# Residual scale and shift deferred through DRAM, and operand sums on VectorE alone

## The chip, the cores and the metric

The kernel runs on one core of one Trainium2 chip. The metric is device time of one execution in microseconds (us); below, the median of three runs. TensorE (PE) multiplies, VectorE (DVE), ScalarE (ACT) and GpSimd (POOL) do elementwise work, SyncE (SP) issues the DMAs.

## The reference, cut to what matters

Two blocks run one after the other over 1024 tokens of width 1024. The change touches the middle of the first (its feed-forward part) and the feed-forward part of the second.

```python
y = hybrid_mixer(h, ...)                      # ends in  o @ w_o
x = layer_norm(ALPHA * x + (1.0 + gt_a) * y, ln1_g, ln1_b)
h = x * (1.0 + sc_f) + sh_f
u = causal_dwconv(h @ w_up, conv_w) + conv_b  # w_up: 1024 x 5632
gate, val = jnp.split(u, 2, axis=-1)
y = (jax.nn.silu(gate) * val) @ w_down
x = layer_norm(ALPHA * x + (1.0 + gt_f) * y, ln2_g, ln2_b)
...
hid = jnp.square(jax.nn.relu(rmsnorm(h, norm_mlp_g) @ w_mlp_in))   # second block
h = h + hid @ w_mlp_out
```

The layer norm's result serves twice: with gain and shift folded into `sc_f` and `sh_f` it is the operand `h` of `w_up`, and scaled by ALPHA it is the residual of the last line of the block.

## The kernel before, in words

All matmuls are fp32, each done as three: an operand is split into a rounded part (hi, a cast) and a remainder (lo, a subtraction), and `mm3` multiplies lo by hi, hi by lo and hi by hi. `split` casts on ScalarE (L430) or VectorE (L432) and subtracts on VectorE (L433) unless told otherwise. Tokens come in two halves of 512; an operand of a half is `op[hf]`, a pair (`oph`, `opl`) of eight slabs of 128x512.

The order of the work comes from generators ("streams") that yield estimated times; `Order` interleaves them, and the tile framework turns what they emit into one in-order queue per engine. Pages of 128x1024 come from an arena; a stream waits with `need` until enough are free.

`out_proj` multiplies by `w_o` and adds the gated result to the residual (`add_gated`: VectorE multiplies, L1716; the add L1717 is GpSimd's for three column blocks of four). After each half it spawns `norm1`: statistics, the normalised row (ScalarE, L642), transposes on TensorE (L419), scale and shift into a buffer (ScalarE, L675) and the split into the operand, all in `to_op`, which has two buffers of half a page and gives the remainder of even slabs to GpSimd. Then `norm1` scales the four rows by `ln1_g` (VectorE, L1761), shifts them by `ln1_b` (GpSimd, L1762), both times ALPHA (L1738), and stores them to `res_d` (L1775). `fix` reads them back in the down stage, hundreds of us later.

`ffn` multiplies by `w_up`. `g_two` does the first two pairs of column blocks in the plain way: products of the first half (op0), then those of the second (op1), with the conv taps L574 on VectorE. The other blocks follow in `st_up` in the manner of Strassen: per two pairs 14 steps of 12 matmuls ("a round"), seven products p = 1, 2, 5, 6, 7, 3, 4, each of two pairs. Products 5, 6, 7 and 4 use sums of the quarters of h, which `x_ops` makes: `ts[0]` (p = 5, step 4), `ts[1]` (p = 6), and two more, called t3 and t4 here (p = 7 and 4), which replace the spare weight ring and a part of op1. Each step's weight is split just ahead, four steps in hand (L433, `wl`). When p = 3 and p = 4 are added up (L1959, L1961), the conv taps of the pair (ScalarE L2088, VectorE L2090 and L2062) and the recombination L1998 to L2001 follow on VectorE, and SyncE stores the result (L2003, L2004). `mlp` of the second block makes its sums with `x_ops` as well.

`x_ops` before: per group of slabs GpSimd takes the hi parts (L1793, L1798, L1802), VectorE the lo parts (L1794, L1795, L1799, L1803) and the remainders.

Of the kernel before, what the change touches and what calls it, by code (L numbers as in the profile page):

```python
# [10 lines left out]
F32 = mybir.dt.float32  # L11
# [3 lines left out]
OP = mybir.AluOpType  # L15
# [4 lines left out]
P = 128  # L20
T = 1024
D = 1024
# [288 lines left out]
class Kern:  # L311
# [348 lines left out]
    def to_op(self, srcs, op, sc, bi=None, kts=range(KT)):  # L660
# [4 lines left out]
        for i, k in enumerate(kts):  # L665
# [3 lines left out]
            if bi is None:  # L669
                nc.scalar.activation(h[:, k, :n], ps[:, :n], AF.Copy, scale=sc(k))  # L670
                nc.vector.scalar_tensor_tensor(l[:, k, :n], ps[:, :n], sc(k), h[:, k, :n].bitcast(F32), op0=OP.mult,
                                               op1=OP.subtract)
            else:
                f = self.opf[i % len(self.opf)]
                nc.scalar.activation(f[:, :n], ps[:, :n], AF.Identity, scale=sc(k), bias=bi(k))  # L675
                self.split(f[:, :n], h[:, k, :n], l[:, k, :n], hi_eng=nc.vector, lo_eng=nc.vector if i % 2 else nc.gpsimd)
            self.psg(ps)
# [1033 lines left out]
    def add_gated(self, hf, c):  # L1711
        def f(t0, ps):
            V, G = self.nc.vector, self.nc.gpsimd
            y = self.yt[:, 4 * hf + t0:4 * hf + t0 + 2, c * 256:(c + 1) * 256]
            t = p3(self.gy[c % 2].ap, 256)[:, t0:t0 + 2]
            V.tensor_tensor(t, ps, self.gt[:, None, c * 256:(c + 1) * 256].to_broadcast([P, 2, 256]), OP.mult)  # L1716
            (V if c == 3 else G).tensor_tensor(y, t, y, OP.add)  # L1717
        return f

    def out_proj(self):  # L1720
# [7 lines left out]
        for hf in range(2):  # L1728
# [4 lines left out]
            if hf == 0:  # L1733
                yield self.need(2)
                self.l1 = A.full(self.ypages), A.full(self.ypages)
                for r, n in zip(self.l1, ("ln1_g", "ln1_b")):
                    self.row_of(r.ap, I[n][0])
                    G.tensor_scalar(r.ap, r.ap, ALPHA, None, op0=OP.mult)  # L1738
                hs = self.const.tile([P, 8], F32, name="h2s")
# [9 lines left out]
    def norm1(self, hf):  # L1749
# [3 lines left out]
        yield from self.ln_rows(rows)  # L1753
        yield self.need(0, 2)
        of = A.half(), A.half()
        self.opf = [h.ap for h in of]
        yield from self.to_op(rows, self.op[hf], lambda k: hs[:, k:k + 1], lambda k: hb[:, k:k + 1])
        self.o.set(self.h2[hf])
        A.give(*of)
# [5 lines left out]
        if hf:  # L1765
            A.give(*self.l1)

# [9 lines left out]

    def x_ops(self, ready, free, evs):


        V, G, A = self.nc.vector, self.nc.gpsimd, self.A
# [4 lines left out]
        t3, t2 = [], []  # L1786
        for j in range(4):
            h11, l11, h12, l12 = [f(x[:, j]) for x in (h0, l0, h1, l1)]
            h22, l22 = f(h1[:, 4 + j]), f(l1[:, 4 + j])
            yield self.need(0, 2)  # L1790
            ap, bp = A.half(), A.half()
            a, b = ap.ap, bp.ap
# [3 lines left out]
            yield 0.4  # L1796
            self.split(a, self.ts[0][0][:, j], self.ts[0][1][:, j])
            G.tensor_tensor(b, h22, a, sub)  # L1798
            V.tensor_tensor(b, b, l22, add)  # L1799
            yield 0  # L1800
            self.split(b, self.ts[1][0][:, j], self.ts[1][1][:, j])
            G.tensor_tensor(a, b, h11, sub)  # L1802
            V.tensor_tensor(a, a, l11, sub)  # L1803
            t3.append(ap)
            t2.append(bp)
            yield 1.54
        yield free
        h3, l3 = [t.rearrange("p (k n) -> p k n", n=512) for t in self.wring[1 - self.wi % 2]]
        for j in range(4):
            self.split(t3[j].ap, h3[:, j], l3[:, j], lo_eng=G if j % 2 else V)  # L1810
            A.give(t3[j])
            yield 1.67
        self.o.set(evs[0])
        for j in range(4):
            b = t2[j].ap
            G.tensor_tensor(b, f(h0[:, 4 + j]), b, sub)
            V.tensor_tensor(b, b, f(l0[:, 4 + j]), add)
            self.split(b, h1[:, j], l1[:, j])
            A.give(t2[j])
            yield 2  # L1820
        self.o.set(evs[1])
# [228 lines left out]
    def ffn(self, sc):  # L2050
# [70 lines left out]
        yield self.h2[0]  # L2121
        self.o.spawn(self.x_ops(self.h2[1], two, tev))
        parts = []
# [958 lines left out]
    def main(self):  # L3082
        G = self.nc.gpsimd
        with ExitStack() as sc:
            ps = self.inner(sc, "pa", 9)
            self.mx = sc.enter_context(self.pool("mx"))
# [3 lines left out]
            self.hgain = self.const.tile([P, 2], F32, name="hgain")  # L3090
            self.x2_d = self.dram.tile([T, D], F32, name="x2_d")
            self.res_d = self.dram.tile([T, D], F32, name="res_d")
            self.g_d = self.dram.tile([32, P, T], F32, name="g_d")
# [74 lines left out]
```

## Time and profile before

| | us |
|---|---|
| median of three runs | 2745.09 (2742.69 to 2749.76) |
| the profiled execution | 2746.61 |
| its span | 2744.9 |
| PE busy | 2585.3 (94%), 13053 matmuls |
| DVE busy | 1972.6 (72%) |
| ACT busy | 1316.8 (48%) |
| POOL busy | 528.3 (19%) |

The span is what the trace covers; the profiled execution's own time holds 1.7 us around it. The granted TensorE clock was 0.982 of full speed over the span. Shares over the span are means over stages: read a stage from windows of it, and a wait from the engine that ended it.

### The profile page before, as it was taken

How to read it: one execution, taken by the hardware profiler on the slowest of the kernel's cores; microseconds unless marked ns; L12 is line 12 of the kernel's file. 1: busy time of each engine (PE TensorE's matmuls, PEld its weight loads, DVE VectorE, ACT ScalarE, POOL GpSimd, SP SyncE). 2: the span in 40 equal slices, each digit the busy share in tenths (PEclk: the TensorE clock that was granted, in tenths of full speed). 3: DMA queues.
4: the chain of work that ended last, by engine and by line, in shares of the span. 5: the costliest groups of instructions: out<-in, count | busy, mean ns of one | idle time of the engine just before them, and what ended most of it. 6: DMA issues, size and time to landing. Idle time of an engine off the chain costs nothing.

```text
span 2744.9 us, 36015 instructions
## 1 busy us (share of the span) xinstructions
PE 2585.3 (94%) x13053; PEld 2100.3 (77%) x13053; DVE 1972.6 (72%) x3200; ACT 1316.8 (48%) x2261; POOL 528.3 (19%) x536
## 2 busy tenths in 40 slices
PE   6889999999789999999989999999999999999998
PEld 4677888789567777788867666679877788888886
DVE  7975565466897877897977686775545867788775
ACT  4434445344244444554356867774444333344443
POOL 4623243335620000000041142320002200000002
PEclk9999999999899999999999999999999999999999
DMA  7423323564323233274410221255304255484541
GB/s 225 158 54 95 84 81 98 161 217 161 118 75 115 70 103 115 81 238 127 161 70 26 82 62 48 63 167 174 122 31 138 85 169 170 146 295 145 170 126 62
DMA packets 290915, 335.57 MB, mean 122 GB/s; under 512 B 32145, under 2 KB 217257, under 8 KB 290737
## 3 DMA queue, kind: packets, MB, share of 16 engines
q1 hardware_dynamic: 290352, 333.12, 38.3%
q8 instruction: 103, 1.69, 0.3%
q14 instruction: 75, 0.61, 0.1%
q10 hardware_dynamic: 385, 0.15, 0.0%
HBM read 239.93 MB, written 89.09 MB: 120 GB/s over the span
## 4 chain that ended last, share of the span: by engine, by line
PE 64%; DVE 19%; ACT 5%; POOL 4%; issue 4%; DMA 3%; SPq 0%; DVEq 0%; POOLq 0%; ACTq 0%
PE b L415 61%; PE b L419 3%; DVE wl L433 2%; DVE y L2090 1%; POOL smalls L597 1%; DVE wf L2090 1%; DVE pg L2090 1%; DVE y L2062 1%; DMA pg<-in_w_ada_dram 1%; DVE y L574 0%; DVE tsl L433 0%; ACT wh L430 0%; POOL y L883 0%; DVE pg L574 0%; DVE y L2029 0%
## 5 line engine op out<-in xcount | busy, mean ns | idle before, releaser
L415 PE MATMUL b<-oph,wl 128*128 128x512 f32 (+1 forms) x1552 | 625.7, 404 | 24.2 <-DVE wl L433 13.8
L415 PE MATMUL b<-opl,wh 128*128 128x512 f32 (+1 forms) x1552 | 615.8, 397 | 8.1 <-DVE opl L433 4.6
L415 PE MATMUL b<-oph,wh 128*128 128x512 f32 (+1 forms) x1552 | 612.0, 395 | 0.0
L415 PEld LDWEIGHTS b<-oph,wl 128*128 128x128 f32 x1552 | 295.0, 190 | 92.9 <-issue 12.0
L415 PEld LDWEIGHTS b<-opl,wh 128*128 128x128 f32 x1552 | 294.6, 190 | 73.1 <-DVE opl L433 5.7
L415 PEld LDWEIGHTS b<-oph,wh 128*128 128x128 f32 x1552 | 294.3, 190 | 63.8 <-issue 2.3
L415 PE MATMUL b<-opl,oph 128*128 128x512 f32 x672 | 261.4, 389 | 0.0
L415 PE MATMUL b<-oph 128*128 128x512 f32 x672 | 261.4, 389 | 0.0
L415 PE MATMUL b<-oph,opl 128*128 128x512 f32 x672 | 261.3, 389 | 0.0
L430 ACT CAST oph<-pg 128x512 fp32r<-128x512 f32 (+1 forms) x204 | 126.8, 629 | 237.9 <-PE b L415 202.4
L415 PE MATMUL b<-wh,opl 128*128 128x256 f32 (+1 forms) x608 | 198.1, 326 | 0.9 <-DVE opl L433 0.6
L415 PE MATMUL b<-wl,oph 128*128 128x256 f32 (+1 forms) x608 | 193.5, 318 | 0.0
L415 PE MATMUL b<-wh,oph 128*128 128x256 f32 (+1 forms) x608 | 193.3, 318 | 0.0
L433 DVE TENSOR_TENSOR opl<-pg,oph 128x512 fp32r<-128x512 f32 x202 | 143.8, 720 | 64.9 <-ACT oph L430 64.3
L430 ACT CAST wh<-y 128x512 fp32r<-128x512 f32 x176 | 109.3, 623 | 137.3 <-PE b L415 114.5
L433 DVE TENSOR_TENSOR wl<-wf,wh 128x1024 fp32r<-128x1024 f32 (+2 forms) x92 | 131.5, 1429 | 56.3 <-ACT wh L430 56.1
L433 DVE TENSOR_TENSOR wl<-y,wh 128x512 fp32r<-128x512 f32 x176 | 121.3, 692 | 69.9 <-ACT wh L430 69.6
L430 ACT CAST wh<-wf 128x1024 fp32r<-128x1024 f32 (+2 forms) x92 | 108.6, 1181 | 81.3 <-PE b L415 42.9
L415 PEld LDWEIGHTS b<-oph 128*128 128x128 f32 x672 | 126.1, 188 | 26.4
L415 PEld LDWEIGHTS b<-oph,opl 128*128 128x128 f32 x672 | 126.1, 188 | 26.2 <-ACT wf L1965 0.2
L415 PEld LDWEIGHTS b<-opl,oph 128*128 128x128 f32 x672 | 126.1, 188 | 26.1
L596 POOL TENSOR_SCALAR rsv<-smalls 128x4 f32<-128x4 f32 (+3 forms) x45 | 12.8, 283 | 645.4 <-DVE smalls L606 591.8
(1092 smaller groups left out, 5373.9 us busy)
## 6 DMA issues: line engine op xcount, KB each, us to landing
pg<-s_d SPq DMA_DIRECT2D x168, 256.0 KB
wf<-in_w_in_dram SPq DMA_DIRECT2D x48, 512.0 KB
y<-in_ffn_w_up_dram SPq DMA_DIRECT2D x30, 512.0 KB
s_d<-y SPq DMA_DIRECT2D x25, 512.0 KB
s_d<-pg SPq DMA_DIRECT2D x22, 512.0 KB
y<-in_w_mlp_in_dram SPq DMA_DIRECT2D x21, 512.0 KB
pa<-in_w_ada_dram SPq DMA_DIRECT2D x41, 256.0 KB
s_d<-wf SPq DMA_DIRECT2D x18, 512.0 KB
```

The source lines that it names most:

```text
L415: self.nc.tensor.matmul(o, a, b, start=start, stop=stop, **kw)
L419: self.nc.tensor.transpose(o, a, self.ident if ident is None else ident)
L430: nc.scalar.copy(hi, src)
L433: (lo_eng or nc.vector).tensor_tensor(out=lo, in0=src, in1=hi.bitcast(F32), op=OP.subtract)
L596: nc.gpsimd.tensor_scalar(v[:, :n], var, EPS, None, op0=OP.add)
L597: nc.gpsimd.tensor_tensor(out, v[:, :n], self.mhalf[:, :n], OP.pow)
L2062: V.tensor_mul(t.ap, a.ap, t.ap)
L2090: V.scalar_tensor_tensor(t[:, d:], x[:, :T - d], tap(2 - d, m), t[:, d:], op0=OP.mult, op1=OP.add)
```

## The change

Residual: `norm1` no longer scales, shifts and stores the residual to `res_d`. It stores the normalised rows to a new DRAM tensor `xh_d` and gives their pages back. A new stream, `res_rows`, starts when `x_ops` has set its second event; it loads the two rows of ln1 (scaled by ALPHA on GpSimd), then per row of tokens loads `xh_d`, scales and shifts it on VectorE in halves (L1784, L1786) and stores it to `res_d`.

Operand sums: for the second half `norm1` takes four pages of the pool `pa`, so each of the eight slabs has its own buffer, and keeps these values before the split. `x_ops` takes two of the four quarters unsplit from there; six VectorE operations a group make the four sums, with no hi and lo parts to add for those quarters. In the second block, where nothing is kept, two more VectorE operations add hi and lo. `to_op`, `add_gated` and `x_ops` use GpSimd no more.

```diff
# to_op
-                self.split(..., hi_eng=nc.vector, lo_eng=nc.vector if i % 2 else nc.gpsimd)
+                self.split(..., hi_eng=nc.vector)
# add_gated
-            (V if c == 3 else G).tensor_tensor(y, t, y, OP.add)
+            V.tensor_tensor(y, t, y, OP.add)
# out_proj: the load and ALPHA scaling of ln1_g, ln1_b (L1734 to L1738) goes
# norm1
+        if hf:
+            yield 5
+            yield self.need(4)
+            of = [A.full(self.pa) for _ in range(4)]
+            self.opf = self.xf = [p.ap[:, c:c + 512] for p in of for c in (0, 512)]
+            self.xfp = of
...
-        for i, x in enumerate(rows):
-            nc.vector.tensor_tensor(x, x, self.l1[0].ap, OP.mult)
-            nc.gpsimd.tensor_tensor(x, x, self.l1[1].ap, OP.add)
-            self.spill(4 * hf + i)
-            yield 8
+        for t in range(4 * hf, 4 * hf + 4):
+            nc.sync.dma_start(self.xh_d[t * P:(t + 1) * P, :], self.yrow(t))
+            A.give(self.ypages[t])
+    def res_rows(self, ready):
+        nc, A, V = self.nc, self.A, self.nc.vector
+        yield ready
+        yield self.need(3)
+        l1 = A.full(), A.full()
+        for r, n in zip(l1, ("ln1_g", "ln1_b")):
+            self.row_of(r.ap, self.I[n][0])
+            nc.gpsimd.tensor_scalar(r.ap, r.ap, ALPHA, None, op0=OP.mult)
+        for t in range(8):
+            yield self.need(1)
+            pg = A.full()
+            x, rows = pg.ap, slice(t * P, (t + 1) * P)
+            nc.sync.dma_start(x, self.xh_d[rows, :])
+            yield 7
+            for c in range(2):
+                cs = slice(c * 512, (c + 1) * 512)
+                V.tensor_tensor(x[:, cs], x[:, cs], l1[0].ap[:, cs], OP.mult)
+                yield 3.5
+                V.tensor_tensor(x[:, cs], x[:, cs], l1[1].ap[:, cs], OP.add)
+                yield 3.5
+            nc.sync.dma_start(self.res_d[rows, :], x)
+            A.give(pg)
# x_ops, per group j
-            G.tensor_tensor(a, h12, h11, sub)
-            V.tensor_tensor(b, l12, l11, sub)
-            V.tensor_tensor(a, a, b, add)
+            if kept:
+                x12, x22 = kept[j], kept[4 + j]
+                V.tensor_tensor(t, x12, h11, sub)
+            else:
+                V.tensor_tensor(x12, f(h1[:, j]), f(l1[:, j]), add)
+                V.tensor_tensor(x22, f(h1[:, 4 + j]), f(l1[:, 4 + j]), add)
+                V.tensor_tensor(t, x12, h11, sub)
+            V.tensor_tensor(t, t, l11, sub)
...
-            G.tensor_tensor(b, h22, a, sub)
-            V.tensor_tensor(b, b, l22, add)
-            G.tensor_tensor(a, b, h11, sub)
-            V.tensor_tensor(a, a, l11, sub)
+            V.tensor_tensor(x12, x22, x12, sub)
+            V.tensor_tensor(t, x22, t, sub)
+            V.tensor_tensor(x22, h21, t, sub)
+            V.tensor_tensor(x22, x22, l21, add)
...
-            self.split(t3[j].ap, h3[:, j], l3[:, j], lo_eng=G if j % 2 else V)
+            self.split(t3[j], h3[:, j], l3[:, j])
...
-            G.tensor_tensor(b, f(h0[:, 4 + j]), b, sub)
-            V.tensor_tensor(b, b, f(l0[:, 4 + j]), add)
# ffn
-        self.o.spawn(self.x_ops(self.h2[1], two, tev))
+        self.o.spawn(self.x_ops(self.h2[1], two, tev, self.xf))
+        self.o.spawn(self.res_rows(tev[1]))
```

VectorE's queue at the end of the out-projection, before: `y` are the residual's rows, `pa_106` is the scaled `ln1_g`, `st` holds the statistics.

```order
L1761 TENSOR_TENSOR y<-y,pa_106 128x1024
L1716 TENSOR_TENSOR pa_104<-b_76,gt 128x512
L1761 TENSOR_TENSOR y<-y,pa_106 128x1024
L1717 TENSOR_TENSOR y<-pa_104,y 128x2x256
L433 TENSOR_TENSOR wl_74<-wf,wh_73 128x2048
L633 BN_STATS st_5324<-y 128x6
```

The same place of the same queue after the change:

```order
L1716 TENSOR_TENSOR pa_104<-b_76,gt 128x512
L1717 TENSOR_TENSOR y<-pa_104,y 128x2x256
L633 BN_STATS st_5322<-y 128x6
L633 BN_STATS st_5326<-y 128x6
L634 BN_AGGR smalls<-st_5322 128x2
L433 TENSOR_TENSOR wl_74<-wf,wh_73 128x2048
L634 BN_AGGR smalls<-st_5326 128x2
```

The scale of the residual no longer stands between the gated add and the statistics, and the weight split stands behind the statistics rather than ahead of them.

TensorE's queue in `g_two`, before: `b3` is a bank of the first pair that takes op1 (`oph1`), `b4` one of the second pair that takes op0.

```order
L419 MATMUL b4_79<-ident_89,y_83 128x128 x4
L415 MATMUL b3_78<-opl1_69,wh0_4027 128x512
L415 MATMUL b7_82<-pg_84,ones_87 1x512
L415 MATMUL b3_78<-oph1_68,wh0_4027 128x512
...
L415 MATMUL b3_78<-opl1_69,wh0_4027 128x512
L415 MATMUL b4_79<-oph0_66,wl1_74 128x512
```

The same place after the change:

```order
L419 MATMUL b4_79<-ident_89,y_83 128x128 x4
L415 MATMUL b0_75<-oph0_66,wh0_4028 128x512
...
L415 MATMUL b3_78<-oph1_68,wl0_4029 128x512
L415 MATMUL b4_79<-oph0_66,wl1_74 128x512
...
L415 MATMUL b6_81<-oph0_66,wh1_73 128x512
L415 MATMUL b3_78<-opl1_69,wh0_4028 128x512
```

Before, products that need op1 stand between and behind the last transposes, ahead of those of the second pair that need op0 alone; after, the 48 products of the second pair (`b4`, `b6`) stand ahead of all but one of them.

VectorE's queue in the first round, before: L1998 to L2001 recombine a pair, L433 with `wl` splits the weights of the next steps, L1952 and L1959 add up products.

```order
L2001 TENSOR_TENSOR pg<-y,wf 128x512
L433 TENSOR_TENSOR wl_4028<-y,wh_4027 128x512
L1952 TENSOR_TENSOR pg<-b_78,pg 128x512
L433 TENSOR_TENSOR wl_4028<-y,wh_4027 128x512 x2
L433 TENSOR_TENSOR wl_4028<-pb_5431,wh_4027 128x512
```

The same place after the change (L2029, L1980 and L1987 are then the numbers of L2001, L1952 and L1959):

```order
L2029 TENSOR_TENSOR pg<-y,pg 128x512
L433 TENSOR_TENSOR wl_4029<-pb_5412,wh_4028 128x512
L1980 TENSOR_TENSOR wf<-b_78,wf 128x512
L1784 TENSOR_TENSOR y<-y,wf 128x512 x2
L433 TENSOR_TENSOR wl_4029<-y,wh_4028 128x512
L1987 TENSOR_TENSOR pg<-b_81,pg 128x512
L433 TENSOR_TENSOR wl_4029<-pb_5413,wh_4028 128x512
L1786 TENSOR_TENSOR y<-y 128x512 x2
L1987 TENSOR_TENSOR pg<-b_82,pg 128x512
```

The four adds of a deferred row (L1784 twice, L1786 twice) stand between the weight splits that TensorE's next steps read.

## Rows read from the trace of the kernel before

**Rows 1.** the page's first part: busy us, share of the span, instructions

```profile
PE 2585.3 (94%) x13053; PEld 2100.3 (77%) x13053; DVE 1972.6 (72%) x3200; ACT 1316.8 (48%) x2261; POOL 528.3 (19%) x536
```

**Rows 2.** 20-us windows: length, busy (x) of PE, PEld, DVE, ACT, POOL; clock, DMA, GB/s

```profile
660.00:680.00 20.00, 20.00 (x172) 20.00 (x171) 12.67 (x17) 7.41 (x8) 9.29 (x7) 1.00 0.35 107
...
700.00:720.00 20.00, 8.59 (x42) 6.60 (x42) 10.73 (x10) 6.86 (x7) 8.35 (x8) 0.74 0.33 106
...
740.00:760.00 20.00, 17.29 (x70) 13.87 (x69) 20.00 (x18) 6.99 (x12) 14.32 (x9) 0.91 0.86 238
```

**Rows 3.** the same view: 690.8 to 834, and the round behind it

```profile
690.80:834.00 143.20, 110.09 (x446) 84.54 (x444) 127.89 (x150) 55.17 (x78) 62.22 (x33) 0.90 0.29 92
834.00:875.50 41.50, 39.00 (x168) 31.37 (x168) 31.90 (x43) 19.01 (x28) 0.00 (x0) 1.00 0.30 96
```

**Rows 4.** TensorE's matmuls of 686 to 694: duration ns, first and last start

```profile
L415 PE MATMUL b<-oph,wl x5: 389/389/396, 690.8 to 693.5; 128*128 128x512 f32 x5
```

**Rows 5.** the chain of waits, 766 to 836: start, us, what

```profile
788.14 0.66 DVE wf L574
...
812.17 0.63 ACT wh L430
...
823.92 0.60 DVE wl L433
824.52 1.19 DVE y L2090
...
826.32 1.14 DVE y L2062
...
830.51 0.46 issue
...
834.05 2.13 PE b L415 x8
```

**Rows 6.** TensorE's waits, 690 to 835: us in total, times, longest

```profile
PE b L415 <- DVE wl L433: 12.4, 4, 6.7
PE b L419 <- ACT y L642: 9.6, 1, 9.6
```

**Rows 7.** the chain of waits from 684 to 716

```profile
697.23 2.88 DVE y L1717
...
704.38 1.27 DVE st L633 x2
...
707.85 1.25 ACT y L642
...
709.14 1.12 PE b L419 x4
```

**Rows 8.** VectorE's groups by line, 690 to 800

```profile
L1761 DVE TENSOR_TENSOR y<-y,pa 128x1024 f32<-128x1024 f32 x7 | 14.9, 2127 | 0.0
...
L433 DVE TENSOR_TENSOR opl<-pg,oph 128x512 fp32r<-128x512 f32 x4 | 5.9, 1484 | 0.0
```

**Rows 9.** GpSimd's groups by line, 640 to 800

```profile
L1762 POOL TENSOR_TENSOR y<-y,pg 128x1024 f32<-128x1024 f32 x8 | 22.4, 2809 | 7.3 <-DVE y L1761 7.3
```

**Rows 10.** VectorE's casts L432, 684 to 740

```profile
L432 DVE CAST oph<-pg x8: 412/1127/1497, 714.9 to 734.2; 128x512 fp32r<-128x512 f32 x8
```

**Rows 11.** ScalarE's waits, 690 to 740

```profile
ACT pg L675 <- DVE opl L433: 8.6, 3, 3.8
```

**Rows 12.** line L1738, GpSimd's scaling of ln1's rows

```profile
L1738 POOL TENSOR_SCALAR pa<-pa x1: 2814/2814/2814, 606.5 to 606.5; 128x1024 f32<-128x1024 f32 x1
...
L1738 POOL TENSOR_SCALAR pg<-pg x1: 4137/4137/4137, 623.6 to 623.6; 128x1024 f32<-128x1024 f32 x1
```

**Rows 13.** SyncE's waits, 600 to 1000

```profile
SPq L2003 <- DVE y L2062: 113.7, 4, 28.7
...
SPq L1885 <- DMA res_d<-y: 3.7, 2, 2.2
```

**Rows 14.** TensorE's waits, 2040 to 2260, the second block's operand sums

```profile
PE b L415 <- DVE wl L433: 4.4, 2, 2.7
```

More of the change, by code (lines that the diff above doesn't have):

```diff
@@ L1733, in out_proj @@
             if hf == 0:
[L1734 to L1738, printed above, removed]
                 hs = self.const.tile([P, 8], F32, name="h2s")
@@ L1753, in norm1 @@
         yield from self.ln_rows(rows)
-        yield self.need(0, 2)
-        of = A.half(), A.half()
-        self.opf = [h.ap for h in of]
+        if hf:
[5 more added lines that the diff above has]
+        else:
+            yield self.need(0, 2)
+            of = A.half(), A.half()
+            self.opf = [h.ap for h in of]
         yield from self.to_op(rows, self.op[hf], lambda k: hs[:, k:k + 1], lambda k: hb[:, k:k + 1])
         self.o.set(self.h2[hf])
-        A.give(*of)
-        for i, x in enumerate(rows):
-            nc.vector.tensor_tensor(x, x, self.l1[0].ap, OP.mult)
-            nc.gpsimd.tensor_tensor(x, x, self.l1[1].ap, OP.add)
-            self.spill(4 * hf + i)
-            yield 8
-        if hf:
-            A.give(*self.l1)
+        if not hf:
+            A.give(*of)
+        for t in range(4 * hf, 4 * hf + 4):
[23 more added lines that the diff above has]
+            A.give(pg)
+        A.give(*l1)
+        self.res_ready = True
     def spill(self, t):
@@ L1776, in spill, with x_ops @@
         self.A.give(self.ypages[t])
-    def x_ops(self, ready, free, evs):
-        V, G, A = self.nc.vector, self.nc.gpsimd, self.A
+    def x_ops(self, ready, free, evs, kept=None):
+        V, A = self.nc.vector, self.A
         (h0, l0), (h1, l1) = self.op
@@ L1785, in x_ops @@
         yield ready
-        t3, t2 = [], []
+        t3, t4, pages = [], [], []
         for j in range(4):
[L1788 to L1792, printed above, removed]
-            G.tensor_tensor(a, h12, h11, sub)
-            V.tensor_tensor(b, l12, l11, sub)
-            V.tensor_tensor(a, a, b, add)
-            yield 0.4
-            self.split(a, self.ts[0][0][:, j], self.ts[0][1][:, j])
-            G.tensor_tensor(b, h22, a, sub)
-            V.tensor_tensor(b, b, l22, add)
-            yield 0
-            self.split(b, self.ts[1][0][:, j], self.ts[1][1][:, j])
-            G.tensor_tensor(a, b, h11, sub)
-            V.tensor_tensor(a, a, l11, sub)
-            t3.append(ap)
-            t2.append(bp)
-            yield 1.54
+            h11, l11, h21, l21 = [f(x[:, k]) for k in (j, 4 + j) for x in (h0, l0)]
+            yield self.need(0, 1 if kept else 3)
+            tp = A.half()
+            t = tp.ap
+            if kept:
+                x12, x22 = kept[j], kept[4 + j]
+                V.tensor_tensor(t, x12, h11, sub)
+            else:
+                pages += [A.half(), A.half()]
+                x12, x22 = [p.ap for p in pages[-2:]]
+                V.tensor_tensor(x12, f(h1[:, j]), f(l1[:, j]), add)
+                V.tensor_tensor(x22, f(h1[:, 4 + j]), f(l1[:, 4 + j]), add)
+                V.tensor_tensor(t, x12, h11, sub)
+            V.tensor_tensor(t, t, l11, sub)
+            self.split(t, self.ts[0][0][:, j], self.ts[0][1][:, j])
+            yield 1
+            V.tensor_tensor(x12, x22, x12, sub)
+            V.tensor_tensor(t, x22, t, sub)
+            self.split(t, self.ts[1][0][:, j], self.ts[1][1][:, j])
+            yield 1
+            V.tensor_tensor(x22, h21, t, sub)
+            V.tensor_tensor(x22, x22, l21, add)
+            A.give(tp)
+            t3.append(x12)
+            t4.append(x22)
+            yield 1
         yield free
@@ L1814, in x_ops @@
         for j in range(4):
-            b = t2[j].ap
-            G.tensor_tensor(b, f(h0[:, 4 + j]), b, sub)
-            V.tensor_tensor(b, b, f(l0[:, 4 + j]), add)
-            self.split(b, h1[:, j], l1[:, j])
-            A.give(t2[j])
-            yield 2
+            self.split(t4[j], h1[:, j], l1[:, j])
+            yield 1.67
+        A.give(*(self.xfp if kept else pages))
         self.o.set(evs[1])
```

8 lines of the change are left out of this document (4 added, 4 removed).

## The prediction

> **What bounds the kernel now.** The page comes first: TensorE is busy for 94% of the span [rows 1], so a change on another engine pays only where TensorE stops. The windows of 20 us show where that is. From 700 TensorE is down to 8.59 of 20 us, at a granted clock of 0.74, and from 740 VectorE is busy for all 20.00 [rows 2]; from 834 on the kernel settles into rounds of 41.5 us with TensorE at 39.00 [rows 3]. The stretch to look at therefore runs from the first product of g_two, 690.8 [rows 4], to step 4 of the second round at 834.05 [rows 5], called the mark below. TensorE is busy there for 110.09 of 143.20 us [rows 3]: 33 us idle. Its longest waits are for VectorE's weight split L433 (12.4 us) and ScalarE's normalised row L642 (9.6) [rows 6], and the chain of waits shows the second step by step: a VectorE add of 2.88, statistics from 704.38, the ScalarE row at 707.85, transposes at 709.14 [rows 7].
>
> VectorE is full there, but not with useful work. One behind another an add of 128x512 takes 0.60 us and one of 128x1024 takes 1.14 [rows 5]; yet L1761, of the larger size, averages 2.13, and the operand remainder, of the smaller, 1.48 [rows 8]. GpSimd's eight L1762, 2.81 each, run at that time [rows 9].
>
> **The change, part by part.** Before, from the first cast of op1 (714.9 [rows 10]) to the mark, the order has VectorE do 85 adds of 128x512, 8 of 128x1024, 8 casts, 17 taps of about 128x511 and 8 of about 128x1023. At 0.60, 1.14, 0.41, 0.66 and 1.19 [rows 5, 10], with under 1 us of tiny ones, that is 84 + 1 = 85 us of work in 119. The new order has 104, 4, 8, 17 and 8 in the same stretch: 91.5 us. So the change adds 6.5 us of VectorE work here, and takes away the operations of GpSimd beside which the old work was stretched by 34.
>
> *The statistics.* Up to 690.8 nothing moves: TensorE is 20.00 of 20 busy at 660 [rows 2], which covers the 12 gated adds and 4 remainders that VectorE takes over from GpSimd (16 x 0.60 = 9.6 us, where VectorE has 7 of 20 free). If that cover failed, up to 9.6 us would come on top; I take nothing. After the last product VectorE now does two adds and a weight split of 128x2048 before the statistics, 6 x 0.60 = 3.6 us; these start at 694.4 rather than 704.38. From there to the transposes it is 4.76 us as before [rows 7], so 699.2 rather than 709.14.
>
> *op1.* The first cast followed the transposes by 5.8 us, so it comes at 705.0. The eight L675 had two buffers and waited 8.6 us for VectorE [rows 11]; with eight half pages that goes, and VectorE's 8 x (0.41 + 0.60) sets the pace: op1 is whole at 713, where before the last cast alone began at 734.2 [rows 10].
>
> *TensorE's way.* g_two has 192 matmuls at 39.00/168 = 0.232 us [rows 3], 44.5 us, and 32 transposes at half of 1.12/4 (that row stands at the lower clock [rows 7]), 4.5 us: from 690.8 that is 739.8. About 2 us are still idle ahead of the transposes, and I take 2 more for the lower clock behind it (before, it was 0.74 after an idle 9.6). The new order puts the 48 second-pair products that need only op0 ahead of all but one of those that need op1, 11 us of cover. g_two ends at 744. Eleven steps of 12 matmuls (2.78 each) lead to 774.6, and the chain from there to the mark is as before, 834.05 - 812.17 = 21.9 [rows 5]: 796.5.
>
> *VectorE's way.* 705.0 + 91.5 = 796.5. By the order, step 0's weight is split after 32 us of this, at 737, and step 4's after 50, at 755; TensorE wants that one at 744 + 4 x 2.78 = 755. Both ways meet, and the mark moves by 834.05 - 796.5 = 37.6 us.
>
> *Costs against it.* Two ways that end together wait for each other in places: 2 us. The two scalings of ln1's rows, 2.81 and 4.14 on GpSimd [rows 12], move from the out-projection into the first round; a few operations behind the second stands the add L1786 that waits for it, and behind that the splits of TensorE's next steps. Beside GpSimd VectorE ran at about half speed (2.13 for 1.14), so 6.95 us of it cost 3.5; from step 4 to the start of the final chain VectorE has 16 us of work in 19.6, which leaves hardly anything; I take 2, with 0 to 7 as the bounds. The Trainium skill (SBUF — State Buffer, "Who interferes with whom") says more: VectorE and GpSimd share a port pair that is locked for a whole instruction, and the loser fully blocks, if a VectorE operation with two SBUF inputs meets a GpSimd one that reads. By that rule all 6.95 us would be lost to VectorE, and the sum below would be 5 us nearer to zero; the trace's L1761, longer by 1.0 us beside operations of 2.81, bears out a part of it only.
>
> The deferred scale and shift is 32 adds, 19.2 us, four of which are counted in the 91.5. The others lie in the next six rounds. A round has 41.5 - 31.9 = 9.6 us without VectorE work [rows 3], all in the half that TensorE bounds, and the order puts nearly all of the adds there: the bounds are 0 and 28 x 0.60 = 16.8, and I take nothing. Each row comes back from DRAM: SP issues its load behind the stores of the round, VectorE stops at L1784 until it lands, and the splits of the next steps wait behind it. TensorE has three prepared steps, 8.3 us, in hand meanwhile. SP's wait of up to 2.2 us for a store of the same size [rows 13] is the nearest row; with 0 to 2.2 for each of six rows I take 0.5, 3 us in all.
>
> In the second block x_ops gets 14 more VectorE operations (8.4 us) and loses GpSimd beside it; TensorE waits for VectorE there for 4.4 us in all [rows 14]. Between -4.4 and +8.4 I take +1, as both effects are of one size. The gate row's store and load beside the first round: +1, 0 to 2.2 by the same store.
>
> Sum: -37.6 + 2 + 2 + 3 + 1 + 1 = -28.6. The profiled run took 2746.6 (a span of 2744.9 and 1.7 around it), which gives 2718.0; the median of the runs is 1.5 lower: 2716.5, written as 2716.
>
> **The rivals.** *VectorE's chains cost their latency.* In the new x_ops each operation reads the one before. The chain of waits has 0.46 us of issue ahead of an operation whose input was just written (at 830.51) [rows 5]. If 24 of the 32 pay it, VectorE's way is 11 us longer, and the sum is -17.6: 2727. For it: VectorE's way has no slack. Against it: the new order interleaves the groups.
>
> *The deferred adds fall on the bounding chain.* In the half of a round that VectorE bounds, 16.8 us come back, and 4 more in the second block: -28.6 + 20.8 = -7.8, 2737. For it: two of the eight rows (the fifth and sixth) stand where the fourth round turns into that half. Against it: the other six stand among the splits of the other half.
>
> *Nothing is won.* If the 34 us of stretch were not GpSimd's doing but waits that stay, VectorE's 6.5 us of new work make the mark that much later: 2752. For it: VectorE is busy 20.00 of 20. Against it: 2.13 beside GpSimd, 1.14 without. The Trainium skill (Perfetto Trace Analysis, "Optimizing Scalar/DVE Operations") holds that offloading from a saturated VectorE, even to GPSIMD, may make sense, which speaks against this change; it adds that the shared read port may spoil that, and the trace sides with the addition.
>
> *Slower: the loads stop VectorE.* VectorE and SP's queue work in order. If each deferred row's load is late by more than the 8.3 us in hand, TensorE stops at every row. Eight such stops undo the gain and 8.2 us more (45.8 in all) once each costs 5.7 us; at 8 us each the sum is 64 - 36 = +28: 2773. For it: SP spends 113.7 us in waits for one VectorE line ahead of its stores, 28.7 at the longest [rows 13], and the row's load stands behind those stores. Against it: the load is queued ahead of its adds by several splits, and a store of its size was done within 2.2 us.
>
> **How the numbers follow.** A measurement here tells 0.3%, 8.2 us, from no change: 2737 to 2753 is "the same". The forecast (2707 to 2722) has 0.54; the latency (2722 to 2732) 0.21; the deferred adds on the chain (2732 to 2742) 0.13, 0.09 of it below 2737; nothing won 0.07; slower by the loads 0.05. So faster 0.84, the same 0.11, slower 0.05. The range: without any cost and with -2 in the second block it is 2706, the low end; 2738 above takes in most of the deferred adds' case.
>
> **What would show it.** Right: the first transposes near 699 and a wait for L642 under 3 us; no 128x512 add of VectorE above 0.8 us from 690 to 740; step 4 of the first round near 755 and the mark near 800; TensorE idle for under 8 us from 690.8 to the mark; rounds of 41.5 us behind it. Wrong: gaps of 0.4 us between the x-sums and a TensorE wait for their remainders (tsl) or for L433 at step 4; rounds above 42 us with L1784 behind a DMA; VectorE waiting for GpSimd's scaling; or late weight loads, since the deferred rows hold three pages of the arena up to the seventh round.

## The result and the profile after

The changed kernel takes 2701.86 us (median of 4 runs, 2694.74 to 2714.76) against 2745.45 for the kernel before (4 runs): ratio 0.9845, interval 0.9806 to 0.9885. The forecast was 2716 with a range from 2706 to 2738: the direction is right, the gain is larger than the range allows. Two repeats of five runs each on other chips, given under the experiments, narrow it: 2691.76 against 2740.81 (0.9827, 0.9810 to 0.9844) and 2691.54 against 2740.45 (0.9824, 0.9811 to 0.9838). The gain is 49 us; the forecast had 29.

The four runs lie 20 us apart, the slower ones at a lower mean granted clock (2694.74 us at 0.989, 2700.91 and 2702.82 at 0.985, 2714.76 at 0.981); a mean lower by 0.008 over 2693 us is 43 us at the lower of the two levels (1.2 of 2.4 GHz), and work at half speed loses half of that, 21.5 us, so the clock would be enough for the spread, though only the fastest of the four has a trace.

The page after, first part, to be held against [rows 1]:

```profile
PE 2569.3 (95%) x13053; PEld 2094.2 (78%) x13053; DVE 1954.4 (73%) x3264; ACT 1317.6 (49%) x2261; POOL 413.4 (15%) x472
```

TensorE does the same 13053 matmuls. So the two executions can be laid side by side by counting matmuls: number 3830 is near the end of the out-projection, 3849 the first of `g_two`, 4077 the first of `st_up` (a step has 12), 4293 the mark, and the ends of the seven rounds behind it follow every 168; 10560 to 10620 is the start of the second block's up stage. The same view of windows as [rows 2, 3], with the stretch from 692.1 (where g_two starts) to the mark, which now stands at 796.6, and the second and third round behind it:

```profile
700.00:720.00 20.00, 19.31 (x98) 14.81 (x99) 14.42 (x29) 11.01 (x15) 0.00 (x0) 1.00 0.87 261
740.00:760.00 20.00, 17.23 (x72) 13.83 (x71) 20.00 (x35) 7.55 (x13) 0.00 (x0) 0.95 0.20 68
692.10:796.60 104.50, 100.15 (x446) 80.70 (x445) 90.79 (x149) 53.41 (x75) 7.57 (x6) 0.98 0.40 124
837.00:879.30 42.30, 39.19 (x169) 31.19 (x167) 37.08 (x50) 20.27 (x30) 0.00 (x0) 1.00 0.37 127
879.40:917.90 38.50, 38.50 (x169) 31.60 (x169) 33.53 (x48) 17.92 (x26) 0.00 (x0) 1.00 0.40 133
```

The stretch shrank from 143.2 us [rows 3] to 104.5, with 4 us of TensorE idle in it instead of 33, though VectorE does one operation less only (149 for 150): its busy time fell from 127.89 to 90.79. From 700 to 720, where TensorE had worked 8.59 us at a clock of 0.74 [rows 2], it works 19.31 at 1.00. The rounds behind it are no longer alike: one takes 42.3, the next 38.5.

The chain of waits at the end of the out-projection, as [rows 7]:

```profile
692.33 0.70 DVE pa L1716
...
693.05 0.70 DVE y L1717
...
693.78 0.80 DVE st L633 x2
...
699.39 1.25 ACT y L642
...
700.68 0.65 PE b L419 x4
```

The gated add takes 0.70 where it took 2.88, the statistics start 1.45 us behind the start of the last gated multiplication L1716, and the transposes at 700.68, 8.6 us behind the first g_two product (the forecast had 8.4). TensorE's waits from 690 to 800, as [rows 6], are two:

```profile
PE b L415 <- issue: 2.8, 1, 2.8
PE b L419 <- ACT y L642: 1.6, 1, 1.6
```

The first of them is step 4's. The profile names no releaser for it, but the step starts at 756.56, 0.1 us behind the end of the VectorE weight split that starts at 755.77, which points to that split:

```profile
755.77 0.69 DVE L433 TENSOR_TENSOR wl<-y,wh 128x512 fp32r<-128x512 f32 x1
```

In the second block (2045 to 2130, as [rows 14]) TensorE waits for nothing any more. The windows of matmuls 10560 to 10620, before and then after:

```profile
2158.60:2179.00 20.40, 16.02 (x61) 12.26 (x60) 16.49 (x21) 8.11 (x16) 4.88 (x3) 0.92 0.33 119
```

```profile
2113.10:2127.10 14.00, 14.00 (x62) 11.28 (x62) 11.45 (x19) 6.89 (x14) 0.00 (x0) 1.00 0.40 111
```

TensorE's time by stretch, from the starts of the numbered matmuls in the traces of the kernels that the next section tells of (the last column is the second block's):

| kernel | median, us (before on that chip) | 3830 to mark | seven rounds | 10300 to 10620 |
|---|---|---|---|---|
| before | 2745.45 | 145.5 | 290.5 | 77.2 |
| changed | 2701.86 (2745.45) | 106.8 | 285.6 | 69.9 |
| changed, repeats | 2691.76 (2740.81), 2691.54 (2740.45) | 105.4, 105.4 | 288.2, 287.4 | 69.9, 69.9 |
| sums changed, residual in place | 2727.66 (2740.81) | 136.3 | 290.5 | 69.9 |
| the same, shift on VectorE | 2717.59 (2739.62) | 127.0 | 290.6 | 69.9 |
| residual deferred, sums as before | 2712.72 (2741.36) | 119.6 | 286.3 | 77.1 |
| before, three pages held | 2729.97 (2740.81) | 141.7 | 282.0 | 77.2 |
| changed, no deferred adds | 2691.02 (2741.36) | 106.7 | 286.1 | 69.9 |
| changed, GpSimd reads, first block | 2708.03 (2741.36) | 121.8 | 287.1 | 69.9 |
| changed, GpSimd writes only | 2691.60 (2739.62) | 108.3 | 284.8 | 69.9 |
| changed, GpSimd reads, second block | 2713.89 (2741.36) | 108.1 | 286.1 | 90.4 |
| changed, old sums on VectorE, second block | 2690.36 (2740.45) | 105.5 | 288.1 | 69.9 |
| changed, pages held throughout | 2688.85 (2740.45) | 105.5 | 280.6 | 69.9 |

The gain is thus 39 to 40 us up to the mark, 2 to 5 in the rounds and 7.3 in the second block; elsewhere the traces differ by up to 4 us either way.

### The profile page after: what moved, and what is told of

The parts are those of the page before. It is cut to its first block, busy times and chain, and to the rows that moved or that the text cites. A ratio compares the mean times of both kernels' runs of the same rounds, so it can differ in the third digit from the quotient of the medians.

```text
span 2693.0 us, 35990 instructions
## 1 busy us (share of the span) xinstructions
PE 2569.3 (95%) x13053; PEld 2094.2 (78%) x13053; DVE 1954.4 (73%) x3264; ACT 1317.6 (49%) x2261; POOL 413.4 (15%) x472
## 3 DMA queue, kind: packets, MB, share of 16 engines
q8 instruction: 103, 1.69, 0.3%
## 4 chain that ended last, share of the span: by engine, by line
PE 70%; DVE 13%; ACT 5%; POOL 4%; DMA 3%; issue 3%; SPq 0%; POOLq 0%; DVEq 0%; ACTq 0%
PE b L415 67%; PE b L419 3%; DVE wl L433 2%; POOL smalls L597 1%; DVE pg L2118 1%; DVE y L2118 1%; ACT wh L430 0%; POOL y L883 0%; DVE y L574 0%; DMA pa<-in_w_ada_dram 0%; DVE wf L2118 0%; DMA wf<-in_w_o_dram 0%; DMA pg<-in_w_ada_dram 0%; POOL rsv L596 0%; DVE y L2057 0%
## 5 line engine op out<-in xcount | busy, mean ns | idle before, releaser
L433 DVE TENSOR_TENSOR opl<-pg,oph 128x512 fp32r<-128x512 f32 (+1 forms) x210 | 144.1, 695 | 64.0 <-ACT oph L430 62.4
L433 DVE TENSOR_TENSOR wl<-wf,wh 128x1024 fp32r<-128x1024 f32 (+2 forms) x98 | 132.8, 1355 | 63.6 <-ACT wh L430 63.4
L430 ACT CAST wh<-y 128x512 fp32r<-128x512 f32 x164 | 101.9, 622 | 127.5 <-PE b L415 108.9
L433 DVE TENSOR_TENSOR wl<-y,wh 128x512 fp32r<-128x512 f32 x164 | 112.7, 691 | 49.3 <-ACT wh L430 48.9
L415 PEld LDWEIGHTS b<-wh,opl 128*128 128x128 f32 x608 | 116.4, 192 | 11.1 <-issue 2.2
```

The lines of the kernel that those rows point to most:

```text
L415: self.nc.tensor.matmul(o, a, b, start=start, stop=stop, **kw)
L430: nc.scalar.copy(hi, src)
L433: (lo_eng or nc.vector).tensor_tensor(out=lo, in0=src, in1=hi.bitcast(F32), op=OP.subtract)
```

## The experiments

The theory after the result: the stretch gained what was forecast, because VectorE is rid of GpSimd beside it; the rounds gained because three held pages change the order; the second block gained for the reason of the first. The rival: the new formula, the fewer waits for GpSimd, or the missing work of VectorE do it.

**The changed kernel again.**

> The changed kernel again, to size the gain and to see whence its runs differ by 20 us (2694.7 to 2714.8). Theory (granted clock): the runs differ only in how many stretches TensorE spends at the lower of its two clock levels; a run 10 us slower shows a mean granted clock lower by 0.004, and its profile, laid beside the first one matmul by matmul, differs only where the clock is lower. Median near 2701, ratio to before 0.984. Rival (the loads of the deferred rows or SyncE's queue vary): the difference sits between 760 and 1010, at a like clock.

Measured: 2691.76, ratio 0.9827 (0.9810 to 0.9844); its runs go from 2690.78 at 0.988 to 2700.72 at 0.986. The trace agrees with the first one to 0.1 us in five of the seven rounds. It differs where the first one has one more spell at the lower level (105.4 against 106.8 in the stretch), where it has one itself (45.5 against 44.0 in the sixth of the seven), and, at a clock of 1.00 in both, in the first round (41.4 against 40.4; 40.7 in the second repeat). So the clock is most of the difference, not all of it. The median came out 9 us lower than expected.

**Three pages held in the kernel before.**

```diff
+    def hold(self, ready):
+        A = self.A
+        yield ready
+        yield self.need(3)
+        ps = [A.full() for _ in range(3)]
+        yield 230
+        A.give(*ps)
...
+        self.o.spawn(self.hold(tev[1]))
```

> The kernel before, with one thing added: a stream takes three pages of the arena when the operand sums are done and gives them back some six rounds later, doing nothing with them. Theory (pages set the order): in the order, the weight splits of the next steps then stand two to four VectorE operations earlier in the half of a round that VectorE bounds, so six rounds shrink from 41.5 to about 39.8 us; 10 us faster than before, about 2735. Rival (the rounds of the changed kernel are shorter because of the deferred adds or of what is loaded): no change, within 2 us of before.

Measured: 2729.97, ratio 0.9958 (0.9945 to 0.9972), 10.8 us faster. The first five of the seven rounds take 39.5 us, the sixth, in which the pages are given back, 43.2, the last 41.5. TensorE's waits from 828 to 1026 are the first row below, and of before from 834 to 1042 the second:

```profile
PE b L415 <- ACT pg L1965: 3.4, 5, 0.7
```

```profile
PE b L415 <- DVE wl L433: 14.2, 11, 1.7
```

The wait for the weight splits is gone, with no work taken away (VectorE is busy for 31.6 to 31.8 us a round, as before, 31.90 [rows 3]). VectorE's rows show how. In the kernel before, from the first add-up L1961 of a round on, its fourth and fifth split of weights (`wl`) and what stands around them are

```profile
812.17 0.69 DVE L1961 TENSOR_TENSOR pg<-b,pg 128x512 f32<-128x512 f32 x1 [1.32 <-PE b L415]
...
826.24 1.22 DVE L2062 TENSOR_TENSOR y<-pg,y 128x1024 f32<-128x1024 f32 x1
...
828.57 0.69 DVE L433 TENSOR_TENSOR wl<-pb,wh 128x512 fp32r<-128x512 f32 x1
...
830.97 1.22 DVE L2062 TENSOR_TENSOR y<-pg,y 128x1024 f32<-128x1024 f32 x1
...
833.31 0.69 DVE L433 TENSOR_TENSOR wl<-y,wh 128x512 fp32r<-128x512 f32 x1
```

and with the pages held, with L1969 and L2070 for L1961 and L2062,

```profile
809.29 0.69 DVE L1969 TENSOR_TENSOR pg<-b,pg 128x512 f32<-128x512 f32 x1 [1.32 <-PE b L415]
...
820.38 0.69 DVE L433 TENSOR_TENSOR wl<-pb,wh 128x512 fp32r<-128x512 f32 x1
...
825.18 0.68 DVE L433 TENSOR_TENSOR wl<-y,wh 128x512 fp32r<-128x512 f32 x1
825.79 1.22 DVE L2070 TENSOR_TENSOR wf<-pg,wf 128x1024 f32<-128x1024 f32 x1
```

The fifth split stood behind the taps and both multiplications of 128x1024, 21.1 us behind the first add-up; now it stands ahead of the first of them, 15.9 us behind it. The changed kernel has the same order at the end of five of its eight rounds (the one that ends at the mark, and the first, third, fourth and fifth of the seven behind it). The rival is out. With fewer free pages the planner takes up the next pair's weights at another moment; that this reorders the splits is shown, the way through the planner's rules was not followed.

**The residual back in place.**

```diff
-        for t in range(4 * hf, 4 * hf + 4):
-            nc.sync.dma_start(self.xh_d[t * P:(t + 1) * P, :], self.yrow(t))
+        for i, x in enumerate(rows):
+            nc.vector.tensor_tensor(x, x, self.l1[0].ap, OP.mult)
+            nc.gpsimd.tensor_tensor(x, x, self.l1[1].ap, OP.add)
+            self.spill(4 * hf + i)
...
-        self.o.spawn(self.res_rows(tev[1]))
```

> The changed kernel with the residual's scale (VectorE) and shift (GpSimd) back in norm1, as before; the operand sums and all other edits as changed. Theory (both halves matter): the transposes come at 705 to 709 again, eight adds of 128x1024 stretched by eight of GpSimd's stand in VectorE's full stretch, so about 8 x 1.14 plus the stretch of 22 us of GpSimd's work, some 20 us, come back there; the rounds are 41.5 again (three pages are no longer held), 8 us; in all 2725 to 2732. Rival (the operand sums are all of it): within 5 us of the changed kernel.

Measured: 2727.66, ratio 0.9952 (0.9939 to 0.9966). 136.3 us to the mark, rounds of 41.5, and the second block keeps its gain. The time is as the theory has it; the stretch gives back 31 us where 20 were expected, the rounds 2 to 5 where 8 were.

**The residual deferred alone**, on the kernel before.

> The kernel before with the residual's deferral alone: scale and shift in the first feed-forward's up stage from DRAM; operand sums, gated adds and remainders with GpSimd as before, two buffers in norm1. Theory (each half of the change has its own share): the mark comes 27 us earlier (what the changed kernel loses when the residual is put back in place), six rounds are shorter by 2 us less what the later ones cost, 5 in all, nothing in the second block: 32 us faster than before, about 2709. Rival (the two halves only work together, since GpSimd's part of the sums still stretches VectorE): 15 us or less.

Measured: 2712.72, ratio 0.9898 (0.9883 to 0.9913): 28.6 us. The stretch gives 25.9 of it, the rounds 4.2, the second block nothing. The two halves alone take 9.2 and 25.9 us off the stretch, together 39 to 40, so each helps the other by 4 to 5. The deferral's share holds that of the three pages too: its last seven steps before the mark take 19.0 us, as with pages held on the kernel before, where the kernel before itself takes 22.1.

**GpSimd work added beside the first block's sums.** A first try, without any operand to wait for, gave nothing on the question:

> The changed kernel with 48 multiplications of 128x256 on GpSimd, on a tile of their own that nobody reads, from the time that op1 is ready (713). Nobody waits for them. Theory (contention): VectorE's adds of 128x512 beside them rise from 0.60 to 1.0 or more for some 30 us; as VectorE's way has no slack in that stretch, the first steps of st_up come 10 to 18 us later. Rival (what mattered was the waits for GpSimd's results, or the number of operations): VectorE's adds stay near 0.60 and the time within 3 us of the changed kernel.

The 48 multiplications ran from 4.8 to 49.2 us, at the start of the program, where they cost 26.1 us (2717.84 against 2691.76 on the same chip); the stretch was free of them. The second try reads a slab of op1:

```diff
+    def noise(self, ready, n, gap):
+        G = self.nc.gpsimd
+        yield ready
+        x = self.op[1][0].bitcast(F32)[:, 7, 0:256]
+        for _ in range(n):
+            G.tensor_tensor(self.nz, x, x, OP.mult)
+            yield gap
...
+        self.o.spawn(self.noise(self.h2[1], 48, 0.65))
```

> The changed kernel with 48 multiplications of 128x256 on GpSimd that read a slab of op1 (two inputs) and write a tile nobody reads, so that they start when op1 is ready, 713. Theory (contention): VectorE's adds of 128x512 beside them rise from 0.60 to 1.0 or more for some 30 us, and as VectorE's way has no slack there, step 0 of st_up and the mark come 10 to 18 us later. Rival (the number of operations and the waits for GpSimd's results were what mattered): adds near 0.60, within 3 us of the changed kernel.

Measured: 2708.03, 16 us above the changed kernel; 121.8 us to the mark, 15 to 16 more. Rows of VectorE from 716 to 760 in that run, then of GpSimd's line:

```profile
L433 DVE TENSOR_TENSOR tsl<-pg,tsh 128x512 fp32r<-128x512 f32 x4 | 4.3, 1072 | 0.0
...
L1830 DVE TENSOR_TENSOR pg<-y,pg 128x512 f32<-128x512 f32 x2 | 2.2, 1113 | 0.0
```

```profile
L1856 POOL TENSOR_TENSOR nz<-oph x48: 613/942/4914, 709.7 to 760.4; 128x256 f32<-128x256 f32 x48
```

The same rows of the changed kernel, from 712 to 766:

```profile
L433 DVE TENSOR_TENSOR tsl<-pg,tsh 128x512 fp32r<-128x512 f32 x4 | 2.8, 689 | 0.1
...
L1830 DVE TENSOR_TENSOR pg<-y,pg 128x512 f32<-128x512 f32 x2 | 1.4, 684 | 0.0
```

An add rises from 0.69 to 1.1 us and GpSimd's own operation from 0.61 to 0.94, with nobody waiting for GpSimd. That is contention and nothing else, and it alone gives back 15 us. VectorE's taps L574, which read one of their inputs from PSUM, stay at 0.74.

**The same with operations that only write.**

```diff
         x = self.op[1][0].bitcast(F32)[:, 7, 0:256]
+        G.tensor_tensor(self.nz, x, x, OP.mult)
         for _ in range(n):
-            G.tensor_tensor(self.nz, x, x, OP.mult)
+            G.memset(self.nz, 1.0)
...
-        self.o.spawn(self.noise(self.h2[1], 48, 0.65))
+        self.o.spawn(self.noise(self.h2[1], 96, 0.35))
```

> The changed kernel with 96 memsets of 128x256 on GpSimd from the time that op1 is ready, which write the same tile as the multiplications did and read nothing. Theory (it is the reading side that VectorE and GpSimd share; the Trainium skill, SBUF — State Buffer, 'Who interferes with whom', holds that an add of two inputs contends with a GpSimd operation that reads, not with one that only writes): adds of 128x512 stay at 0.60 to 0.70, the mark within 2 us of the changed kernel. Rival (any work on GpSimd slows VectorE): adds near 1.1 as beside the multiplications, the mark some 10 us later.

Measured: 2691.60, ratio 0.9824, as the changed kernel; 108.3 us to the mark. GpSimd, then VectorE's adds from 716 to 745:

```profile
L1857 POOL MEMSET nz<- x96: 311/312/318, 714.6 to 749.7; 128x256 f32 x96
```

```profile
L433 DVE TENSOR_TENSOR tsl<-pg,tsh 128x512 fp32r<-128x512 f32 x4 | 2.7, 683 | 0.0
```

30 us of GpSimd work leave VectorE's adds at 0.68. The rule of the Trainium skill (SBUF — State Buffer, "Who interferes with whom") holds here: an add of two inputs meets GpSimd's reads, not its writes. That the loser fully blocks is what single rows of the kernel before show. GpSimd's, then VectorE's:

```profile
753.02 1.61 POOL L1802 TENSOR_TENSOR pg<-pg,oph 128x512 f32<-128x512 f32 x1 [1.29 <-DVE pg L1799]
```

```profile
752.80 0.68 DVE L1794 TENSOR_TENSOR y<-opl,opl 128x512 f32<-128x512 f32 x1
753.40 1.77 DVE L1794 TENSOR_TENSOR pg<-opl,opl 128x512 f32<-128x512 f32 x1
```

The add that starts ahead of GpSimd's operation takes 0.68; the one that starts during it ends at 755.17, 0.54 behind the other's end. In the run with the multiplications the two engines take turns: from 719 to 736 a multiplication and an add end once each in every 1.02 us. So the factors of 1.5 to 1.6 are those of waiting for the other's turn. A part of each still runs beside the other: alone, one behind another, an add takes 0.60 and a multiplication 0.69.

How much of this the stretch holds can be summed. Against the median duration of the same operation and shape without GpSimd beside it, VectorE's operations from matmul 3830 to the mark are longer by 33.2 us in the kernel before, 18.0 with the deferral alone, 16.0 with the residual in place, 15.5 beside the multiplications, and by 1.0 in the changed kernel. The rival that waits for GpSimd's results did it is small there: from 690 to 834 of the kernel before VectorE waits for none, TensorE for 2.0 us.

**The residual in place, without GpSimd.**

> The run with the residual back in norm1, but its shift on VectorE too, so that GpSimd has nothing beside VectorE there: 8 more adds of 128x1024 for VectorE. Theory (contention is most of what the residual in place costs): TensorE's way from matmul 3830 to the mark takes 112 to 120 us (105.4 of the changed kernel plus up to 16 x 1.14 on VectorE's way, less what fits into its idle time ahead of op1), against 136.3 with GpSimd; 2705 to 2713. Rival (it is the place of these operations ahead of the statistics and of op1): 132 or more, no gain over the run with GpSimd.

Measured: 2717.59, ratio 0.9923 (0.9906 to 0.9940); 127.0 us to the mark, between the two expectations. L1769 there takes 1.20 (it was 1.88 with GpSimd's shift beside it), and TensorE's wait for L642 falls from 11.2 to 4.9:

```profile
PE b L415 <- DVE wl L433: 13.4, 4, 7.0
PE b L419 <- ACT y L642: 4.9, 1, 4.9
```

The windows from matmul 3830 to the mark, with GpSimd's shift and then without:

```profile
687.40:823.70 136.30, 110.35 (x465) 88.09 (x464) 118.23 (x163) 54.71 (x78) 25.74 (x12) 0.90 0.31 100
```

```profile
687.10:814.10 127.00, 108.25 (x465) 86.82 (x463) 109.67 (x169) 54.85 (x78) 5.36 (x4) 0.92 0.32 106
```

The 9.3 us between the two are not the whole of the contention: VectorE has eight adds more here (8 x 1.14 is 9.1) and is still busy for 8.6 us less. The sum over its operations says the same, 16.0 us longer than alone with GpSimd's shift and 0.2 without it. So of the 31 us that the residual in place costs in the stretch, about half are contention. Of the rest, the eight scalings (another 9.1) and the pages that are no longer held (3.0, in the last seven steps before the mark) are the nearest terms, and some 3 us stay open. The theory, that contention is most of it, is right for about half.

**The deferred adds left out.**

```diff
-                V.tensor_tensor(x[:, cs], x[:, cs], l1[0].ap[:, cs], OP.mult)
                 yield 3.5
-                V.tensor_tensor(x[:, cs], x[:, cs], l1[1].ap[:, cs], OP.add)
```

> The changed kernel without the 32 adds of the deferred scale and shift; rows of the normalised residual are loaded and stored as they are (the output lacks ln1's gain, shift and ALPHA in the residual). Theory (the adds lie in the half of a round that TensorE bounds): within 2 us of the changed kernel, 2690 to 2694. Rival (they cost their 0.6 us each somewhere): up to 19 us faster, 2673.

Measured: 2691.02, as the changed kernel. Four rounds of it, then the same four of the changed kernel:

```profile
831.40:991.10 159.70, 155.16 (x674) 125.76 (x673) 127.32 (x169) 76.45 (x112) 0.00 (x0) 1.00 0.38 129
```

```profile
837.00:996.70 159.70, 155.19 (x673) 125.75 (x672) 138.88 (x189) 76.43 (x112) 0.00 (x0) 1.00 0.38 129
```

20 operations and 11.6 us of VectorE more, in the same 159.70 us: there the adds cost nothing. In the first of the seven rounds, ahead of these four, they, or the load that they wait for, cost 1 to 2 us: 39.4 without them, 40.4 to 41.4 in the three traces of the changed kernel.

**The second block.** GpSimd's multiplications beside its sums:

> The changed kernel with the same 48 multiplications beside the operand sums of the second block. Theory (contention made TensorE wait for 4.4 us there before, and its end took 7 us off): VectorE's adds there stretch to 1.0 or more for 30 us, TensorE waits again for the splits ahead of steps 4 and 5, 4 to 8 us are lost. Rival (the new formula makes its sums in an order that suits the steps): within 2 us of the changed kernel.

Measured: 2713.89, 22 us above the changed kernel. 20.5 of it stand in matmuls 10300 to 10620 (90.4 for 69.9), where TensorE waits 13.4 us at once for a split and 2.7 for a sum's cast, and the granted clock is 0.70 over the 34.4 us:

```profile
PE b L415 <- DVE wl L433: 13.4, 1, 13.4
PE b L415 <- ACT tsh L430: 2.7, 1, 2.7
```

```profile
2111.50:2145.90 34.40, 18.35 (x61) 13.83 (x60) 29.75 (x41) 11.91 (x22) 8.94 (x9) 0.70 0.40 138
```

The mechanism is right; the price was more than twice the 8 us that were expected at most. And the old formula without GpSimd:

> The changed kernel, with the second block's operand sums by the formula of before, but with all of its operations on VectorE. Theory (contention is what cost 7 us there): TensorE's way through the start of the up stage (its matmuls 10560 to 10620) takes 14 us, as with the new formula, and the time is that of the changed kernel within 2 us. Rival (the new formula has the sums ready in a better order): 18 to 20 us there, 4 to 7 us slower.

Measured: 2690.36, and 13.9 us for matmuls 10560 to 10620, as with the new formula. There GpSimd was the whole of the 7.3 us; the formula is worth nothing to TensorE. Whether it was contention or VectorE's waits for GpSimd's results this run does not say, as it takes both away: in the kernel before, VectorE waits for such results for 6.0 us from 2100 to 2180. That contention alone can do it is shown by the multiplications, for which nobody waited.

**The pages held in all rounds.** The measure on the same chip, and then the changed kernel with its pages held in all rounds:

> The changed kernel once more, as the measure for the next run on the same chip. Theory: ratio to before 0.981 to 0.984; the runs that stand out are those of a lower granted clock.

```diff
-        for t in range(8):
-            yield self.need(1)
-            pg = A.full()
+        pg = A.full()
+        for t in range(8):
...
-            A.give(pg)
-        A.give(*l1)
+        yield 70
+        A.give(pg, *l1)
```

> The changed kernel with one row page kept for all eight deferred rows and all three pages held until after the last of them and 70 planner-us more, so that the order has the early splits in every round but the last (in the changed kernel the third, the seventh and the last ones have the old order). Theory (pages set the order of the splits): three more rounds lose 1.7 to 2 us each, less some of the deferred adds that now stand in the half that VectorE bounds (up to 4 x 0.6 in two rounds of three): 2 to 5 us faster than the changed kernel. Rival (the rounds of the changed kernel are as short as TensorE's work allows): no change; or slower by 3, if the load of each row must now wait for the store of the row before.

Measured: 2688.85, ratio 0.9811 (0.9798 to 0.9824), against 2691.54 (0.9824) for the changed kernel. The seven rounds take 280.6 us, where the three traces of the changed kernel have 285.6 to 288.2, with a wait for L433 of 0.5 us in all. The two intervals overlap, so the 2.7 us between the medians is not shown by the times alone; the 5 to 8 us in the rounds are what the traces show.

## Why the prediction was wrong

*The stretch.* From matmul 3830 the forecast meant 145.5 - 37.6 = 107.9 us without its costs and 112.9 with them; 105.4 to 106.8 were measured. The transposes came 8.6 us behind g_two's start (8.4; the split of 128x2048 stands behind the statistics, not ahead of them as the prediction counts it, which leaves the sum as it is). By the forecast TensorE takes 53.2 us for g_two, 11.1 to step 4, 19.5 to step 11 and 21.9 from there to the mark; it took 50.6, 13.8, 21.0 (19.7 in the repeats, which have no spell at the lower clock there) and 19.0. So the mark at 796.6, for 796.5 and the 1.3 by which this run is late at 690, is right in part by luck: errors cancel. Of *costs against it* the first came: TensorE waited 2.8 us at step 4, where the two ways meet and 2 were taken. The 2 for ln1's scaling and the 1 for the gate row did not, nor the 2 for a lower clock behind the transposes: it was granted in full there. The scaling did stop VectorE, as said: it waited 1.2 and 2.7 us for the two scalings, the second of which had waited 2.8 for its row. TensorE, with its steps in hand, did not notice.

The prediction took L1761's 2.13 as a sign that GpSimd blocks VectorE in part only. That is a mean of seven: three started with no operation of GpSimd under way and took 1.17 to 1.21; four started during one and took 1.69 to 3.40, and each of these ended 1.08 us behind the end of that operation.

*The 19.0 us from step 11 to the mark are the step that failed in kind:* "the chain from there to the mark is as before", and "A round has 41.5". Both took the order of the VectorE-bound half for granted. The order of the changed kernel had the rows; it was read for where the new adds stand, not for where the old splits went. They moved ahead at the end of five of eight rounds, since the deferred rows hold three pages: these last steps take 22.0 to 22.1 us in each trace without held pages (before, and the residual in place with or without GpSimd) and 19.0 to 19.1 in each with them, the kernel before with held pages included. So the deferred rows, put down as +3, are worth -2 to -5 behind the mark: the loads did stop VectorE (2.8, 2.7 and 1.2 us in all rounds together), TensorE by no more than the 1 to 2 us of the first of the seven rounds. The later order gives 2 to 3 us in three rounds; the second and the sixth of the seven, at whose ends the old order comes back, take 42.4 and 44.0 to 45.5. Why the sixth is the longest was not followed.

*The second block* was mis-sized: +1 was taken, within -4.4 and +8.4, and -7.3 came. The step set 8.4 us of more VectorE work against the 4.4 us of waits and took them to be of one size. But the added operations lie beside TensorE's work, and what was late was late by GpSimd. With the waits goes also the spell at the lower clock behind them: 4.4 of waits, 0.9 of another that ended there, and the 1.6 us that a clock of 0.92 over 20.4 us costs.

Together 6 to 8 us in the stretch, 5 to 8 in the rounds and 8 in the second block, 21 to 22 in each of the three traces; between the forecast's -28.6 and -49 lie 20.4. The first measurement's 2701.86 shows 5 us less of the gain; its runs had the lower clock.

*The rivals.* The x-sums' latency: the chain ran without gaps (L1830 at 0.69, none idle before it; VectorE waits for 0.3 us in all from 712 to 766), and the groups are interleaved. The deferred adds on the bounding chain: no more than the 1 to 2 us of the first round, by the run without them. Nothing won: out, by GpSimd's added work. The loads: never later than 2.8 us.

## What to carry to other kernels

Where VectorE sets the end and GpSimd reads beside it, count GpSimd's work as VectorE's (here beside adds and casts, not beside the taps with an input in PSUM): moving it over can be free, and a wait that GpSimd seems to cause may go with it, in every stage that uses the same helper. A mean duration hides this; look at single operations and at what ran beside them. When a change holds or frees buffers, read the new order for what old instructions did in the loops behind it; three idle pages alone were worth 11 us. Price a wait together with the lower clock behind it.

## What the runs showed of the hardware

A GpSimd multiplication of 128x256 (0.61 us alone) and VectorE adds of 128x512 (0.60 one behind another, 0.69 each) stretch one another to 0.94 and 1.1 us, one of each in 1.02; an add that starts during a GpSimd operation of 1.61 us ends 0.54 behind it, and a cast L432 of 0.41 takes up to 1.50 beside GpSimd [rows 10]; taps with an input in PSUM stay at 0.74; a GpSimd memset of the same size (0.31) stretches neither. TensorE's waits of 13.4 and 2.7 us in the second block went with a granted clock of 0.70 over 34.4 us, and cost 20.5. Without any work changed, one kernel's runs differ by up to 20 us, the slower at a lower mean granted clock (0.981 for 0.989).
